# Out projection to MLP in a hybrid decoder block: token tiles one by one, norm gains on DVE, a fixed order on three engines, up blocks two at a time

## Chip, cores and metric

The kernel runs on one core of a Trainium2 chip. The metric is the device time of one execution in microseconds (us). Engines: PE (matmul), DVE (vector), ACT (activation), POOL (GpSimd) and SP, which issues the DMAs.

## What is computed

Two decoder layers on x of 512 tokens by 1024. The stage that the change touches lies between the attention heads and the MLP:

```python
mix = jnp.concatenate([o_fox, o_nsa, o_dil], axis=-1)      # 512 x 1024
x = x + rms_norm(mix @ w_out[l], attn_post_norm[l])
h = rms_norm(x, ffn_pre_norm[l])
x = x + rms_norm(conv_ffn(h, w_up[l], conv_w[l], conv_b[l], w_down[l]), ffn_post_norm[l])

def rms_norm(x, g):
    return x * lax.rsqrt(jnp.mean(x * x, axis=-1, keepdims=True) + RMS_EPS) * g
def conv_ffn(h, w_up, conv_w, conv_b, w_down):
    a, b = jnp.split(causal_depthwise_conv3(h @ w_up) + conv_b, 2, axis=-1)   # 2 x 2816 columns
    return (jax.nn.silu(a) * b) @ w_down
```

## The kernel before

Tokens are worked on in four tiles `s` of 128 (`NST`). Every fp32 matmul is split: an operand is parted into a high half (a copy rounded to fp32r, made by ACT) and a low half (the rest, a subtraction on DVE or POOL), and three products are accumulated: high by high, high by low, low by high.

**Weights.** `plan` lists all weight blocks in order, `getw` (L204) loads (SP) and parts them (`part_weights`, L139) some blocks ahead of use: `ahead` is how far it loads, `pre` how far it parts. Raw blocks, high halves and low halves have three slots each (`wpool`); blocks in `UPS` take their halves from the pool `big` (24 slots of 4 KB per partition), which also holds x, h, the partial out projection `part`, the gains, and the transposed operands `hT`. Blocks in `ONPOOL` are parted in two halves, with POOL for the low half; the others with DVE. An up block (i, n) is 1024 x 128 of w_up; n counts four blocks of one i.

**Out projection.** `part[s]` holds the first half of the heads' products. Four more k (4 to 7) are accumulated in PSUM (`out_mms`, L850): tiles 0 and 1 in the fill of the attention loop, tile 2 and tile 3 at the end (L1207 to L1209). Each tile has two PSUM tiles of 512 columns, `po[s, 0]` and `po[s, 1]`, from four tags ("acc" three banks, "s" two, "pt" two, "o" one).

**Norm and residual.** `mid_post(s)` (L862) loads x for tile s, adds `po` to `part` on DVE (L871) and calls `post_sq` (L275): ACT squares with a row sum (L284), and the gain product h = part x gain (L287) runs on POOL, for all eight halves (`GM1`). `post_r` (L289) and `rstd_of` (L232) give the reciprocal root for a pair of tiles at once: a root on ACT (L234), then on DVE v, a reciprocal, a Newton step (L235 to L243). `post_x` (L300) makes x + h r on DVE (L304) and squares it on ACT (L309). `pre_h` (L311) scales x by its own reciprocal root, on DVE (L322) for all four tiles here (`HA1` is empty) and on ACT (L320) elsewhere for some.

**Turn.** `turn_pair` (L258) transposes two tiles of h on PE (L264; 16 transposes into four PSUM tiles, two k in each), and for each k ACT writes the high half with the pre-norm gain (L269, `hh`) and DVE the low half (L270, `hl`).

**First up blocks.** The four blocks of i = 0 are worked in two halves of 256 tokens (L1230 to L1235): for each pair of k all four blocks in turn, into PSUM tiles acc, acc, s, s; the second turn lies between the halves. The rest of the MLP (L1248 on) takes 512 tokens at a time.

**Order.** Only PE's instructions are held to the program's order (`tc.manual_schedule`, L1183). The order on DVE, ACT, POOL and SP is chosen when the program is built: by what is ready in its scheduler's estimate, with program order as the priority. On the chip each engine then runs its list strictly in that order. So x of tile 3 can be loaded after weights that stand later in the code.

The lines around the change in short:

```python
mid_post(0); mid_post(1); post_r(0); post_x(0); post_x(1)
mid_post(2); pre_h(0, HA1); pre_h(1, HA1)
ws = [getw(l, "up", 0, n, ahead=0) for n in range(2)]
turn_pair(0, 1, l, HT1)
mid_post(3); post_r(1); post_x(2); post_x(3)
ws += [getw(l, "up", 0, n, ahead=UPA[n - 2], pre=UPP[n - 2]) for n in range(2, 4)]
pre_h(2, HA1); pre_h(3, HA1)
```

Of the kernel before, what the change touches and what calls it, by code (L numbers as in the profile page):

```python
# [12 lines left out]
AF = mybir.ActivationFunctionType  # L13
# [5 lines left out]
DM = 1024  # L19
# [10 lines left out]
ONPOOL = ("dv", "dq", "dk", "ks", "nq0", "kw", "kc", "nq1",  # L30
          (0, "fk", 0), (0, "fk", 1), ("up", 0, 1), ("up", 0, 2), ("up", 0, 3), ("up", 1, 0))
PRE = 1
# [11 lines left out]
ORDER = (0, 1, 2, 4, 3, 5, 6, 7, 8)  # L44
GM1 = ((0, 0), (0, 1), (1, 0), (1, 1), (2, 0), (2, 1), (3, 0), (3, 1))
HA0 = (1, 3)
HA1 = ()
XC = 1
# [3 lines left out]
UPS = ((0, 0), (1, 0))  # L52
UPA = (1, 2)
UPP = (0, 1)
HT3 = ("pt", "pt", "acc", "o")
KT = 8


# [18 lines left out]
def tile_hybrid_block(  # L77
# [144 lines left out]
    epsc = const.tile([128, 1], F32, name="epsc")  # L222
    nc.vector.memset(epsc, EPS)
    onec = const.tile([128, 1], F32, name="onec")
# [6 lines left out]

    def rstd_of(total):  # L232
        y, v, t, r = (st(total.shape[-1]) for _ in range(4))
        nc.scalar.activation(y, total, AF.Sqrt, scale=1.0 / DM, bias=epsc)  # L234
        nc.vector.tensor_scalar(v, total, 1.0 / DM, EPS, op0=ALU.mult, op1=ALU.add)  # L235
        nc.vector.reciprocal(y, y)
        if total.shape[-1] == 1:
            nc.vector.scalar_tensor_tensor(t, y, v, y, op0=ALU.mult, op1=ALU.mult)
        else:
            nc.vector.tensor_mul(t, y, v)  # L240
            nc.vector.tensor_mul(t, t, y)
        nc.vector.tensor_scalar(t, t, -0.5, 1.5, op0=ALU.mult, op1=ALU.add)
        nc.vector.tensor_mul(r, y, t)  # L243
        return r

    def new_hT():
# [11 lines left out]
    def turn_pair(half, i, l, tags, tilewise=False):  # L258

        gain = pre_g[:, i, l, :]  # L260
        pts = [ps(tag) for tag in tags]
        order = [(k, i) for k in range(KT) for i in range(2)]
        for k, i in sorted(order, key=lambda z: z[1]) if tilewise else order:
            nc.tensor.transpose(pts[k // 2][:, 256 * (k % 2) + 128 * i:256 * (k % 2) + 128 * i + 128],  # L264
                                hs[2 * half + i][:, 128 * k:128 * k + 128], ident)
        for k in range(KT):
            src = pts[k // 2][:, 256 * (k % 2):256 * (k % 2) + 256]
            hi, lo = (z[k // 2][:, k % 2, 256 * half:256 * half + 256] for z in hT)
            nc.scalar.activation(hi, src, AF.Copy, scale=gain[:, k:k + 1])  # L269
            nc.vector.scalar_tensor_tensor(lo, src, gain[:, k:k + 1], f(hi), op0=ALU.mult, op1=ALU.subtract)  # L270
# [157 lines left out]
    for l in range(DEPTH):  # L428
# [432 lines left out]

        def mid_post(s):  # L862
            if s == 0:
                table(AF.Sqrt, units[-1]["row"][:, 0:1])
            xt = bt([128, DM], name="x")
            nc.sync.dma_start(xt, x[0, 128 * s:128 * s + 128, :] if l == 0 else xsv[128 * s:128 * s + 128, :])
            xs.append(xt)
            y = store["part"][s]
            halves = [y[:, 512 * u:512 * u + 512] for u in range(2)]
            for u in range(2):  # L870
                nc.vector.tensor_add(halves[u], halves[u], po[s, u])  # L871
            post_sq(s, halves, gains[0], GM1)

# [296 lines left out]
        def up_mms(p, w, sl, first, last, ks=range(KT)):  # L1170
            hi, lo = w
            for k in ks:
                mm(p[:, sl], hi[:, k, :], HH(k)[:, sl], first and k == 0, False)
                mm(p[:, sl], hi[:, k, :], HL(k)[:, sl], False, False)
                mm(p[:, sl], lo[:, k, :], HH(k)[:, sl], False, last and k == KT - 1)

# [6 lines left out]
        with tc.manual_schedule(engines={mybir.EngineType.PE}):  # L1183
# [16 lines left out]
            while whole or live[0] or pieces.late:  # L1200
                if whole and store.get("pc"):
                    cmp_values(whole.pop(0)[0])
                elif live[0] or pieces.late:
                    step()
                    chain_step()

            out_mms(2, (7,), True, (0,))  # L1207
            out_mms(2, (4, 5, 6, 7), True, (1,))
            out_mms(3, (4, 5, 6, 7), True)  # L1209
            hT = new_hT()  # L1210
            mid_post(0)
            mid_post(1)
            post_r(0)
            post_x(0)
            post_x(1)
            mid_post(2)
            pre_h(0, HA1)
            pre_h(1, HA1)
            ws = [getw(l, "up", 0, n, ahead=0) for n in range(2)]
            turn_pair(0, 1, l, HT1)  # L1220
            mid_post(3)
            post_r(1)
            post_x(2)
            post_x(3)
            ws += [getw(l, "up", 0, n, ahead=UPA[n - 2], pre=UPP[n - 2]) for n in range(2, 4)]
            pre_h(2, HA1)
            pre_h(3, HA1)
            table(AF.Silu, hs[3][:, 0:1])
            pts = [ps(t) for t in ("acc", "acc", "s", "s")]
            for half in range(2):  # L1230
                if half == 1:
                    turn_pair(1, 1, l, HT3)
                for k in range(0, KT, 2):
                    for n in range(4):
                        up_mms(pts[n], ws[n], slice(256 * half, 256 * half + 256), half == 0, half == 1, (k, k + 1))  # L1235

# [102 lines left out]
```

## Time and profile before

| | us |
|---|---|
| median of 3 runs (lowest to highest) | 1391.84 (1391.26 to 1394.37) |
| the profiled execution, its time | 1393.86 |
| its span, first to last instruction | 1391.9 |
| PE busy | 1341.9 (96%) |
| DVE busy | 869.6 (62%) |
| ACT busy | 725.5 (52%) |
| POOL busy | 316.4 (23%) |

All durations come from the one profiled execution. The stage in question occurs once per layer, in the trace near 314 to 361 us and near 1000 to 1047 us. "Busy" of PE says that matmuls were in flight, not that they ran at full speed; the granted clock of PE is 1.00 at 2.4 GHz and 0.50 at 1.2 GHz. A timeline row gives start, duration, engine, line, operation, output <- inputs, shape and count; a row with a count above one covers several instructions in a row. In brackets stands how long the engine was idle before it, and whose result ended that. In the names, `wh`, `wl` are high and low weight halves (`wh_up`, `wl_up`: those with wpool slots), `sm` small columns of sums and roots.

### The profile page before, as it was taken

Reading aid. Unit: us, or ns where it says so; the run is one execution under the profiler, and the core shown is the slowest. Engines: PE = TensorE matmul, PEld = TensorE weight load, DVE = VectorE, ACT = ScalarE, POOL = GpSimd, SP = SyncE. Lnnn points to the kernel's source line nnn. Section 1 sums busy time; section 2 is a strip of 40 time slices with the busy share of each in tenths; the row PEclk is TensorE's granted clock in tenths of the full one; section 3 lists DMA queues with packets and bytes.
Section 4 is the critical chain, followed back from the end, with each engine's and each line's share of the span. In section 5 each row is a group of like instructions: output and inputs, shape, how many; then the busy total and the mean of one; then the engine's idle time right before and its main releaser. Section 6 shows DMA issues by size and latency. Waiting matters only on the chain.

```text
span 1391.9 us, 21204 instructions
## 1 busy us (share of the span) xinstructions
PE 1341.9 (96%) x7835; PEld 1181.3 (85%) x7835; DVE 869.6 (62%) x2006; ACT 725.5 (52%) x1525; POOL 316.4 (23%) x363
## 2 busy tenths in 40 slices
PE   6999999998999999999999999999989999999997
PEld 5899998977888888888899899999788888888886
DVE  6678877678655555533464887876767555554334
ACT  6567766775443333423465677677655333333232
POOL 2363763345000000000004646633430000000000
PEclk9999999999999999999999999999999999999999
DMA  5224311132233333223323143112323333332231
GB/s 178 77 62 116 102 46 37 54 122 63 77 91 100 98 92 106 91 96 124 117 81 105 47 125 88 32 46 62 106 61 101 96 92 105 91 103 95 91 121 61
DMA packets 145519, 123.75 MB, mean 89 GB/s; under 512 B 8264, under 2 KB 135688, under 8 KB 145416
## 3 DMA queue, kind: packets, MB, share of 16 engines
q1 hardware_dynamic: 145416, 122.40, 29.1%
q8 instruction: 62, 1.02, 0.3%
q14 instruction: 41, 0.34, 0.1%
HBM read 118.19 MB, written 4.19 MB: 88 GB/s over the span
## 4 chain that ended last, share of the span: by engine, by line
PE 80%; DVE 11%; ACT 6%; issue 2%; DMA 0%; POOL 0%; SPq 0%; ACTq 0%; DVEq 0%
PE acc L117 36%; PE s L117 18%; PE pt L117 13%; PE o L117 10%; PE pt L1102 3%; DVE hl L270 1%; DVE wt L772 1%; DVE x L304 1%; DVE pl L1118 1%; DVE r L1077 1%; DVE r L449 1%; ACT r L284 1%; DVE h L322 1%; ACT r L1082 1%; PE pt L714 1%
## 5 line engine op out<-in xcount | busy, mean ns | idle before, releaser
L156 DVE TENSOR_TENSOR wl_up<-raw_up,wh_up 128x1024 fp32r<-128x1024 f32 x78 | 95.6, 1225 | 163.1 <-ACT wh_up L148 163.1
L148 ACT ACTIVATE wh_up<-raw_up 128x1024 fp32r<-128x1024 f32 (+1 forms) x90 | 89.6, 1002 | 154.3 <-PE acc L117 68.1
L156 DVE TENSOR_TENSOR wl_wd<-raw_wd,wh_wd 128x1024 fp32r<-128x1024 f32 x42 | 51.5, 1226 | 133.6 <-ACT wh_wd L148 133.6
L148 ACT ACTIVATE wh_wd<-raw_wd 128x1024 fp32r<-128x1024 f32 x42 | 44.5, 1061 | 144.9 <-PE pt L117 135.5
L1082 ACT ACTIVATE r<-r,sm 128x128 f32<-128x128 f32 x192 | 106.7, 557 | 21.5 <-DVE sm L1077 20.8
L1089 POOL TENSOR_SCALAR r<-r,sm,gates 128x128 f32<-128x128 f32 (+3 forms) x128 | 86.6, 682 | 119.4 <-DVE sm L1087 82.6
L152 POOL TENSOR_TENSOR wl_kc<-raw_kc,wh_kc 128x512 fp32r<-128x512 f32 x8 | 12.0, 1511 | 419.5 <-ACT wh_kc L148 418.7
L117 PE MATMUL acc<-hh,wh_up 128*128 128x512 f32 (+1 forms) x272 | 102.4, 377 | 0.0
L117 PE MATMUL acc<-hl,wh_up 128*128 128x512 f32 (+1 forms) x272 | 102.4, 377 | 0.0
L117 PE MATMUL acc<-hh,wl_up 128*128 128x512 f32 (+1 forms) x272 | 102.4, 376 | 0.0
L117 PE MATMUL s<-k,q 128*128 128x512 f32 (+3 forms) x384 | 96.5, 338 | 2.2 <-DVE sm L1077 0.9
L1118 DVE TENSOR_TENSOR pl<-pt,ph 128x384 fp32r<-128x384 f32 x144 | 85.6, 595 | 16.9 <-ACT ph L1113 15.5
L1113 ACT ACTIVATE ph<-pt 128x384 fp32r<-128x384 f32 x144 | 75.4, 524 | 24.7 <-PE pt L1102 23.1
L1077 DVE CUSTOM_DVE_ANT_0 r<-s,cmask 128x128 f32<-128x128 f32 (+3 forms) x160 | 75.8, 483 | 18.3 <-PE s L117 13.4
L1102 PE MATMUL pt<-ident,r 128*128 128x128 f32 x480 | 77.9, 277 | 7.2 <-DVE pl L1118 5.7
L117 PE MATMUL acc<-wh_wd,gh 128*128 128x512 f32 x252 | 83.7, 389 | 0.0
L117 PE MATMUL s<-hh,wh_up 128*128 128x512 f32 (+1 forms) x224 | 80.6, 360 | 2.2 <-DVE hl L270 2.2
L117 PE MATMUL s<-hl,wh_up 128*128 128x512 f32 (+1 forms) x224 | 80.3, 359 | 0.0
L117 PE MATMUL s<-hh,wl_up 128*128 128x512 f32 (+1 forms) x224 | 80.3, 359 | 0.0
L1263 ACT ACTIVATE r<-r 128x512 f32<-128x512 f32 x44 | 27.8, 633 | 81.3 <-DVE r L1244 81.0
L1102 PEld LDWEIGHTS pt<-ident,r 128*128 128x128 f32 x480 | 55.7, 141 | 16.1 <-POOL r L1089 7.1
L117 PE MATMUL acc<-wh_wo,mix 128*128 128x256 f32 (+1 forms) x296 | 67.5, 305 | 0.0
(431 smaller groups left out, 4187.2 us busy)
## 6 DMA issues: line engine op xcount, KB each, us to landing
raw_up<-in_w_up_dram SPq DMA_DIRECT2D x88, 512.0 KB, 3.8
raw_wd<-in_w_down_dram SPq DMA_DIRECT2D x44, 512.0 KB, 3.4
raw_wo<-in_w_out_dram SPq DMA_DIRECT2D x16, 512.0 KB, 3.4
x<-in_x_dram SPq DMA_DIRECT2D x8, 512.0 KB, 6.5
raw_nq<-in_w_in_dram SPq DMA_DIRECT2D x8, 512.0 KB, 3.6
raw_w<-in_cmp_w_k_dram SPq DMA_DIRECT2D x8, 512.0 KB, 3.7
raw_w<-in_cmp_w_v_dram SPq DMA_DIRECT2D x8, 512.0 KB, 4.2
raw_fk<-in_w_in_dram SPq DMA_DIRECT2D x4, 512.0 KB, 6.8
```

The source lines that it names most:

```text
L117: nc.tensor.matmul(o, lhsT=lhsT, rhs=rhs, start=start, stop=stop, skip_group_check=True)
L148: nc.scalar.activation(hi[:, ks], raw[:, ks], AF.Copy)
L156: nc.vector.tensor_sub(lo[:, ks], raw[:, ks], f(hi)[:, ks])
L270: nc.vector.scalar_tensor_tensor(lo, src, gain[:, k:k + 1], f(hi), op0=ALU.mult, op1=ALU.subtract)
L284: nc.scalar.activation(scr, y, AF.Square, accum_out=stats["p", s // 2][:, c:c + 1])
L1077: nc.vector.tensor_tensor_reduce(row[:, 0:n], u["S"][:, 0:n], u["mask"][:, 512 - n:512], op0=ALU.add, op1=ALU.min, scale=1.0, scalar=3.0e3 ...
L1082: nc.scalar.activation(row[:, 0:n], row[:, 0:n], AF.Exp, scale=-1.0, bias=sm_[:, 0:1], accum_out=sm_[:, 1:2])
L1089: nc.gpsimd.tensor_scalar(row[:, 0:n], row[:, 0:n], sm_[:, 2:3], g_, op0=ALU.mult, op1=ALU.mult)
L1102: nc.tensor.transpose(p[:, 128 * c:128 * c + 128], blocks[z], ident)
L1113: nc.scalar.activation(hi, src, AF.Copy)
L1118: nc.vector.tensor_sub(*u["lo"])
L1263: nc.scalar.activation(cd[0], cd[0], AF.Silu)
```

## The change

The post-norm and pre-norm work is taken tile by tile for tiles 0 and 1, with a sum and a reciprocal root for each tile (tiles 2 and 3 still share the first one); the gain products move from POOL to DVE; h of tiles 0 and 2 is scaled on ACT, of 1 and 3 on DVE. PE, DVE and ACT are held to program order from the last out-projection matmuls to the end of the first four up blocks. Transposes go tile by tile, the evacuation of k goes 0, 2, 1, 3, 4, 6, 5, 7 in every turn of the kernel, and the up matmuls follow that order, blocks 0 and 1 through all k before blocks 2 and 3. The x loads and the h tiles come earlier, the parts of up blocks (0,2) and (0,3) come before the first turn, and block (1,0) is parted by ACT and DVE behind the second turn instead of by POOL. The reciprocal root has one DVE operation fewer everywhere (constants are folded by a factor of four).

```diff
-          (0, "fk", 0), (0, "fk", 1), ("up", 0, 1), ("up", 0, 2), ("up", 0, 3), ("up", 1, 0))
+          (0, "fk", 0), (0, "fk", 1), ("up", 0, 1), ("up", 0, 2), ("up", 0, 3))
...
+KORDER = (0, 2, 1, 3, 4, 6, 5, 7)
...
-    def rstd_of(total):
-        y, v, t, r = (st(total.shape[-1]) for _ in range(4))
-        nc.scalar.activation(y, total, AF.Sqrt, scale=1.0 / DM, bias=epsc)
-        nc.vector.tensor_scalar(v, total, 1.0 / DM, EPS, op0=ALU.mult, op1=ALU.add)
+    def rstd_begin(total):
+
+        y, v = (st(total.shape[-1]) for _ in range(2))
+        nc.scalar.activation(y, total, AF.Sqrt, scale=4.0 / DM, bias=epsc)
+        nc.vector.tensor_scalar(v, total, -4.0 / DM, -4.0 * EPS, op0=ALU.mult, op1=ALU.add)
+        return y, v
+
+    def rstd_end(y, v):
+        t, r = (st(y.shape[-1]) for _ in range(2))
         nc.vector.reciprocal(y, y)
...
-        nc.vector.tensor_scalar(t, t, -0.5, 1.5, op0=ALU.mult, op1=ALU.add)
-        nc.vector.tensor_mul(r, y, t)
+        nc.vector.scalar_tensor_tensor(r, t, 3.0, y, op0=ALU.add, op1=ALU.mult)
         return r
...
-        for k in range(KT):
+        for k in KORDER:
             src = pts[k // 2][:, 256 * (k % 2):256 * (k % 2) + 256]
...
+        def mid_load(s):
             xt = bt([128, DM], name="x")
             nc.sync.dma_start(xt, x[0, 128 * s:128 * s + 128, :] if l == 0 else xsv[128 * s:128 * s + 128, :])
             xs.append(xt)
...
+            hs.append(bt([128, DM], name="h"))
+
+        def mid_add(s, u, square=True):
+
+            y = store["part"][s][:, 512 * u:512 * u + 512]
+            nc.vector.tensor_add(y, y, po[s, u])
+            if square:
+                mid_square(s, u)
+
+        def mid_square(s, u):
+            y = store["part"][s][:, 512 * u:512 * u + 512]
+            nc.scalar.activation(rt(), y, AF.Square, accum_out=mid["p"][:, s % 2 + 2 * (s // 2) + 4 * u:][:, 0:1])
+
+        def mid_gain(s, us=(0, 1)):
+            for u in us:
+                cs = slice(512 * u, 512 * u + 512)
+                nc.vector.tensor_mul(hs[s][:, cs], store["part"][s][:, cs], gains[0][:, cs])
+
+        def mid_total(s, n=1):
+            tot = st(n, "sx")
+            nc.vector.tensor_add(tot, mid["p"][:, s:s + n], mid["p"][:, 4 + s:4 + s + n])
+            return rstd_begin(tot)
+
+        def mid_x(s, r):
+            nc.vector.scalar_tensor_tensor(xs[s], hs[s], r, xs[s], op0=ALU.mult, op1=ALU.add)
+            nc.scalar.activation(hs[s], xs[s], AF.Square, accum_out=mid["x"][:, s:s + 1])
...
+            for s in range(2):
+                mid_load(s)
+            ws = [getw(l, "up", 0, n, ahead=0) for n in range(2)]
+
+
+        table(AF.Sqrt, units[-1]["row"][:, 0:1])
+        mid["p"], mid["x"] = st(8, "sq"), st(4, "sx")
+        for s in range(2, NST):
+            mid_load(s)
+        with tc.manual_schedule(engines={mybir.EngineType.PE, mybir.EngineType.DVE, mybir.EngineType.Activation}):
             out_mms(2, (7,), True, (0,))
             out_mms(2, (4, 5, 6, 7), True, (1,))
             out_mms(3, (4, 5, 6, 7), True)
             hT = new_hT()
...
+            mid_add(0, 0)
+            mid_add(0, 1)
+            mid_gain(0)
+            a0 = mid_total(0)
+            mid_add(1, 0)
+            mid_x(0, rstd_end(*a0))
+            mid_add(1, 1)
+            mid_gain(1)
+            b0 = rstd_begin(mid["x"][:, 0:1])
+            a1 = mid_total(1)
+            nc.scalar.activation(hs[0], xs[0], AF.Copy, scale=rstd_end(*b0))
+            mid_x(1, rstd_end(*a1))
+            mid_add(2, 0)
+            mid_gain(2, (0,))
+            b1 = rstd_begin(mid["x"][:, 1:2])
+            mid_add(2, 1)
+            nc.vector.tensor_scalar(hs[1], xs[1], rstd_end(*b1), None, op0=ALU.mult)
+            ws.append(getw(l, "up", 0, 2, ahead=1, pre=0))
+            ws.append(getw(l, "up", 0, 3, ahead=2, pre=0))
+            mid_add(3, 0, False)
+            mid_add(3, 1, False)
+            mid_gain(2, (1,))
+            turn_pair(0, 1, l, HT1, True)
+            mid_square(3, 0)
+            mid_square(3, 1)
+            mid_gain(3)
+            r = rstd_end(*mid_total(2, 2))
+            mid_x(2, r[:, 0:1])
+            mid_x(3, r[:, 1:2])
+            for s in range(2, 4):
+                r = rstd_of(mid["x"][:, s:s + 1])
+                if s == 2:
+                    nc.scalar.activation(hs[s], xs[s], AF.Copy, scale=r)
+                else:
+                    nc.vector.tensor_scalar(hs[s], xs[s], r, None, op0=ALU.mult)
             table(AF.Silu, hs[3][:, 0:1])
             pts = [ps(t) for t in ("acc", "acc", "s", "s")]
             for half in range(2):
                 if half == 1:
-                    turn_pair(1, 1, l, HT3)
-                for k in range(0, KT, 2):
-                    for n in range(4):
-                        up_mms(pts[n], ws[n], slice(256 * half, 256 * half + 256), half == 0, half == 1, (k, k + 1))
+                    turn_pair(1, 1, l, HT3, True)
+                    getw(l, "up", 1, 0, ahead=1, pre=0, peek=True)
+                for n0 in (0, 2):
+                    for k in range(0, KT, 2):
+                        for n in (n0, n0 + 1):
+                            up_mms(pts[n], ws[n], slice(256 * half, 256 * half + 256), half == 0, half == 1,
+                                   KORDER[k:k + 2])
```

## Rows read from the trace of the kernel before

**Rows 1.** The page, part 4: the chain that ended last, by engine.

```profile
PE 80%; DVE 11%; ACT 6%; issue 2%; DMA 0%; POOL 0%; SPq 0%; ACTq 0%; DVEq 0%
```

**Rows 2.** Windows: length, busy time of each engine (instructions), granted clock, DMA share, GB/s.

```profile
329.40:333.10 3.70, 3.48 (x18) 3.22 (x19) 2.45 (x6) 3.04 (x9) 3.70 (x3) 0.57 0.02 4
...
333.10:344.90 11.80, 10.70 (x87) 10.35 (x87) 10.09 (x20) 6.68 (x15) 6.63 (x6) 1.00 0.59 178
...
332.50:333.00 0.50, 0.50 (x6) 0.50 (x5) 0.50 (x2) 0.50 (x2) 0.50 (x1) 0.93 0.00 0
...
1015.40:1019.10 3.70, 3.47 (x17) 3.22 (x18) 2.44 (x6) 3.04 (x9) 3.70 (x3) 0.56 0.02 4
```

**Rows 3.** Timeline of PE: start, us, operation, count [idle before <- releaser].

```profile
326.76 0.39 PE L117 MATMUL acc<-wh_wo,mix 128*128 128x512 f32 x1
...
329.38 0.45 PE L264 MATMUL pt<-ident,h 128*128 128x128 f32 x1 [2.23 <-DVE h L322]
...
330.04 1.73 PE L264 MATMUL pt<-ident,h 128*128 128x128 f32 x7 [0.22 <-DVE h L322]
...
332.85 0.36 PE L117 MATMUL acc<-hh,wh 128*128 128x256 f32 x1
...
336.63 0.36 PE L117 MATMUL s<-hh,wh_up 128*128 128x256 f32 x1 [0.60 <-DVE hl L270]
...
346.53 0.98 PE L264 MATMUL pt<-ident,h 128*128 128x128 f32 x7 [0.20 <-DVE h L322]
...
360.57 0.40 PE L117 MATMUL pt<-hh,wh 128*128 128x512 f32 x1
```

**Rows 4.** The chain of waits in order of time: start, us, what.

```profile
350.65 1.44 PE s L117 x12
...
1386.28 0.16 DVE sm L242
...
1386.66 1.28 DVE x L304
```

**Rows 5.** Timeline of POOL.

```profile
315.04 5.05 POOL L287 TENSOR_TENSOR h<-part,gain 128x512 f32<-128x512 f32 x4 [9.61 <-DVE part L871]
...
321.64 2.27 POOL L287 TENSOR_TENSOR h<-part,gain 128x512 f32<-128x512 f32 x1 [1.55 <-DVE part L871]
```

**Rows 6.** Timeline of DVE.

```profile
314.26 2.05 DVE L871 TENSOR_TENSOR part<-part,acc 128x512 f32<-128x512 f32 x3 [0.38 <-PE acc L117]
...
318.89 1.22 DVE L235 TENSOR_SCALAR sm<-sm 128x2 f32<-128x2 f32 x1
...
321.48 3.52 DVE L304 SCALAR_TENSOR_TENSOR x<-h,sm,x 128x1024 f32<-128x1024 f32 x2
...
328.48 1.42 DVE L322 TENSOR_SCALAR h<-x,sm 128x1024 f32<-128x1024 f32 x2
...
332.43 0.88 DVE L270 SCALAR_TENSOR_TENSOR hl<-pt,preg,hh 128x256 fp32r<-128x256 f32 x2 [0.16 <-ACT hh L269]
...
364.63 0.68 DVE L1264 TENSOR_TENSOR g<-r,r 128x512 f32<-128x512 f32 x1
```

**Rows 7.** Timeline of ACT.

```profile
318.89 0.30 ACT L234 ACTIVATE sm<-sm,epsc 128x2 f32<-128x2 f32 x1 [1.06 <-DVE sm L293]
...
322.79 1.06 ACT L309 ACTIVATE h<-x 128x1024 f32<-128x1024 f32 x1 [0.47 <-DVE x L304]
...
328.64 1.66 ACT L148 ACTIVATE wh_up<-raw_up 128x512 fp32r<-128x512 f32 x3
...
330.95 0.47 ACT L269 ACTIVATE hh<-pt,preg 128x256 fp32r<-128x256 f32 x1 [0.66 <-PE pt L264]
```

**Rows 8.** Timeline of SP's DMA queue.

```profile
306.94 1.05 SPq L866 DMA_DIRECT2D x<-in_x_dram  x2
...
332.71 0.58 SPq L866 DMA_DIRECT2D x<-in_x_dram  x1
```

**Rows 9.** The page, part 6: DMA issues, KB each, median us to landing.

```profile
raw_up<-in_w_up_dram SPq DMA_DIRECT2D x88, 512.0 KB, 3.8
```

More of the change, by code (lines that the diff above doesn't have):

```diff
@@ L44 @@
 ORDER = (0, 1, 2, 4, 3, 5, 6, 7, 8)
-GM1 = ((0, 0), (0, 1), (1, 0), (1, 1), (2, 0), (2, 1), (3, 0), (3, 1))
 HA0 = (1, 3)
-HA1 = ()
 XC = 1
@@ L52 @@
 UPS = ((0, 0), (1, 0))
-UPA = (1, 2)
-UPP = (0, 1)
 HT3 = ("pt", "pt", "acc", "o")
 KT = 8
+KORDER = (0, 2, 1, 3, 4, 6, 5, 7)
 PAT = ((0,), (2, 1), (4, 5, 3), (6, 9, 7, 8))
@@ L222, in tile_hybrid_block @@
     epsc = const.tile([128, 1], F32, name="epsc")
-    nc.vector.memset(epsc, EPS)
+    nc.vector.memset(epsc, 4.0 * EPS)
     onec = const.tile([128, 1], F32, name="onec")
@@ L230, in table @@
         nc.scalar.activation(t, after, func, scale=0.0, bias=onec)
-    def rstd_of(total):
-        y, v, t, r = (st(total.shape[-1]) for _ in range(4))
-        nc.scalar.activation(y, total, AF.Sqrt, scale=1.0 / DM, bias=epsc)
-        nc.vector.tensor_scalar(v, total, 1.0 / DM, EPS, op0=ALU.mult, op1=ALU.add)
+    def rstd_begin(total):
[5 more added lines that the diff above has]
+        t, r = (st(y.shape[-1]) for _ in range(2))
         nc.vector.reciprocal(y, y)
-        if total.shape[-1] == 1:
+        if y.shape[-1] == 1:
             nc.vector.scalar_tensor_tensor(t, y, v, y, op0=ALU.mult, op1=ALU.mult)
@@ L241, in rstd_of @@
             nc.vector.tensor_mul(t, t, y)
-        nc.vector.tensor_scalar(t, t, -0.5, 1.5, op0=ALU.mult, op1=ALU.add)
-        nc.vector.tensor_mul(r, y, t)
-        return r
+        nc.vector.scalar_tensor_tensor(r, t, 3.0, y, op0=ALU.add, op1=ALU.mult)
+        return r
+    def rstd_of(total):
+        return rstd_end(*rstd_begin(total))
     def new_hT():
@@ L860, in tile_hybrid_block @@
         hs.clear()
-        def mid_post(s):
-            if s == 0:
-                table(AF.Sqrt, units[-1]["row"][:, 0:1])
+        def mid_load(s):
             xt = bt([128, DM], name="x")
@@ L867, in mid_post @@
             xs.append(xt)
[L868 to L872, printed above, removed]
+            hs.append(bt([128, DM], name="h"))
[18 more added lines that the diff above has]
+            nc.scalar.activation(hs[s], xs[s], AF.Square, accum_out=mid["x"][:, s:s + 1])
+        mid = {}
         def out_start():
@@ L1172, in up_mms @@
             for k in ks:
-                mm(p[:, sl], hi[:, k, :], HH(k)[:, sl], first and k == 0, False)
+                mm(p[:, sl], hi[:, k, :], HH(k)[:, sl], first and k == KORDER[0], False)
                 mm(p[:, sl], hi[:, k, :], HL(k)[:, sl], False, False)
-                mm(p[:, sl], lo[:, k, :], HH(k)[:, sl], False, last and k == KT - 1)
+                mm(p[:, sl], lo[:, k, :], HH(k)[:, sl], False, last and k == KORDER[-1])
         RATE = [1.4] * 12 + [0.8] * 98
@@ L1210, in tile_hybrid_block @@
             hT = new_hT()
[L1211 to L1227, printed above, removed]
+            mid_add(0, 0)
[33 more added lines that the diff above has]
+                    nc.vector.tensor_scalar(hs[s], xs[s], r, None, op0=ALU.mult)
             table(AF.Silu, hs[3][:, 0:1])
```

## The prediction

> **What bounds the kernel now.** I read the chain that ended last first: TensorE (PE) holds 80% of the span, DVE 11% and ACT 6% [rows 1]. So a saving counts only where PE waits or runs slowly. Then the stage that the diff touches, cut into windows, once per layer, and PE's timeline in it. The layers agree to 0.1 us (the slow stretch gave PE 3.48 of 3.70 us at a granted clock of 0.57 in one, 3.47 of 3.70 at 0.56 in the other) [rows 2], so I work out layer 0 and take it twice.
>
> The last out-projection matmul starts at 326.76 and ends at 327.15; the first matmul of the next pair of up blocks starts at 360.57 [rows 3]: 33.4 us. The work in it is 192 up matmuls (two halves, 8 k, 4 blocks, 3 products), at 12 in 1.44 us [rows 4] 23.0 us, and 32 transposes, at 7 in 0.98 us [rows 3] at most 4.5 and nearer 4: together 27. About 6.4 us per layer can be won. They go to: 2.23 us before the first transpose, for DVE's h; the clock, which falls to half (1.2 GHz) after that idle time, so that 16 transposes take the 3.70 us window instead of some 2.0; 1.10 us in the window from 333.1 (11.80 long, 10.70 busy) [rows 2], where blocks 2 and 3 wait until DVE has emptied the PSUM tiles that they take over (0.60 us before the second of them); the rest around the two turns (first operands of each half, 0.20 us for h before the second) [rows 3].
>
> Why h is late is in DVE's and POOL's rows. POOL multiplies the norm gains, four in 5.05 us from 315.04 [rows 5]. While it does, tiny DVE operations that take 0.16 us elsewhere [rows 4] take 1.22, and two updates of x, 1.28 each at the kernel's end [rows 4], take 3.52 [rows 6]: they take turns with POOL.
>
> **The change, part by part.** The start is the same: DVE's first addition at 314.26, when PE delivers [rows 6].
>
> *DVE up to h1.* In the new order DVE does, tile by tile: for tile 0 two additions (0.68, three in 2.05) and two gain products (bounded by the same-shaped product of two SBUF operands, 0.68; 1.27, POOL's own time, as the far bound; I take 0.66 in a row, since it is DVE's own row [rows 6]): 2.6; one addition, 0.7; five small ones at 0.2 apart, 1.0; the x update, 1.28; an addition and two products, 2.0; eight small ones, 1.6; an x update, 1.28; two additions and a product of tile 2, 2.0; four small ones, 0.8; h1's scaling, 0.71 (two in 1.42, ending at 329.9 before) [rows 6]. Sum 13.9: h1 at 328.1. ACT's squares (1.06 for a whole tile [rows 7], some 0.6 for half of one, and a short reading of the sum behind each) fall beside it, and h0, which ACT scales in 1.06, is ready near 323.7, not 329.2. No POOL work is left in this stretch, so nothing makes DVE's operations wait; that is where the 5 us that DVE takes over are paid.
>
> *First turn.* PE transposes h0 from 327.2 without a gap, then h1 from about 328.2 to 329.3. ACT's fixed order puts the four weight halves of up blocks 2 and 3 (three in 1.66 [rows 7], so 2.2) after its last square, at 327.4, and ahead of the evacuation, so the first hh starts at 329.7, before 330.95 [rows 7]. With 0.47 for hh and 0.44 for hl (two in 0.88) [rows 6, 7] both operands of the first k stand at 330.6; before, the first up matmul started at 332.85 [rows 3]. The gain is 2.3. Here lies the clock's gain too: PE's longest idle time shrinks from 2.23 to about 1 us, so I take the full clock; at half, 1.7 comes back.
>
> *Evacuation order.* The order that goes round the tiles lets ACT fill the next tile while DVE reads the last. Two blocks a time use a pair of k in 1.44 us, for which ACT and DVE need some 0.9, so PE doesn't starve, and blocks 2 and 3 start 5.8 us later, when their PSUM tiles are long empty. The 1.10 us are gone. Half 0 ends at 330.6 + 95 x 0.12 = 342.0.
>
> *Second half.* Now DVE and ACT are late next. DVE's last hl of half 0 ends near 333.6. Then two gain products, 1.4, with 0.2 for a meeting with POOL's last half (335.2); sum and reciprocal root of both tiles, 1.2; two x updates, 2.56 (339.0); ACT's second square to 340.2; root (0.30 [rows 7]) and three small ones, 0.9; ACT's scaling of h2, 1.06 (342.2); root and small ones for h3, behind it on ACT, 0.9; scaling, 0.71 (343.8); one transposed column block, hh and hl, 1.1: 344.9. PE has transposed h2 by then. End of half 1: 345.0 + 11.5 = 356.5 to 356.6, against 360.57: **4.0 us per layer**, 8.0 for two. Some 2.4 of the 6.4 stay lost.
>
> *Block (1,0).* Its weight part goes from POOL to ACT and DVE, behind the second turn, done by about 350, needed at 356.6: nothing. If that cover went it would cost PE at most the 4.0 gained.
>
> *Loads.* The x loads and the tiles for h come earlier in SP's queue and in the pool; before, two x loads went out at 306.94 and the fourth only at 332.71 [rows 8]. They are needed at 318 to 338: nothing, if slots are free (see the slower rival).
>
> *Reciprocal root.* One small DVE operation fewer wherever it is used. On the chain that is sure at the tail (0.16 and its gap, 0.2 [rows 4]) and at the layer boundary, 0.2; at the start between 0 and 0.4; I take 0.4 in all. The turns elsewhere only change the order of k: between -0.5 and +0.5 by one operand's 0.44 and its gap; I take 0, the middle, for DVE and ACT are not held to program order there.
>
> Sum: 8.0 + 0.4 = 8.4. The profiled execution took 1393.86 us (span 1391.9 and 2.0 around it), so it would take 1385.5. The median of the runs is 2.0 lower, 1391.84, which gives **1383.4**.
>
> **The rivals.** *The clock falls all the same* (15%). Between 327.15 and the first up matmul near 330.2 PE has only transposes, with gaps. If these keep no clock up, PE starts the up matmuls at half speed, and the 1.7 us come back in both layers: 1386.8. Against it: the clock was back within the window from 332.50 (mean 0.93, so by 332.6) [rows 2], when PE had run nothing but transposes since 329.38; the first matmul came at 332.85 [rows 3].
>
> The Trainium skill (TensorE: Matmul & The Clock Gate, Part 4: PE-mode transpose) says that a transpose "doesn't count as PE-busy the same way"; by that rule the time would be this rival's, and the trace disagrees, with the clock back before any matmul.
>
> *The fixed order turns POOL's work into waits* (10%). The parts of blocks 2 and 3 on POOL now run from about 328 to 333.5, and DVE's gain products of tiles 2 and 3 stand ahead of hl and of h2. If each of two meetings costs a whole POOL operation (1.27), 2.5 per layer: 1388.4. For it: the 1.22 us operations. Against: they wait for at most one operation, and POOL is nearly done at tile 3.
>
> *Given back downstream* (8%). If the weights of the second pair of blocks keep their old times, PE waits there for all it won: 1391.4. Against it: blocks 0 and 1 end 5.8 us before the stage does, and free their weight tiles and PSUM earlier.
>
> *Slower: the queue behind x* (5%). The x loads of tiles 2 and 3 now stand ahead of the weights of up blocks 2 and 3. If x3 still finds its slot at 332.71 and SP holds those weights behind it, they issue at 333.3 and 333.8 and land 3.8 later [rows 9], ACT has them parted at 338.7 and hh follows in ACT's order: 9.0 late, less the 4.0, is 5.0 per layer slower, 1401.4. It decides once the last weights land after 334. Against it: before, three h tiles had slots by 321.7 [rows 5], which is enough for h0, h1 and x3 now.
>
> **How the numbers follow.** Forecast 62%. A measurement of this kernel tells about 0.2% (2.8 us) from no change. Faster: forecast, clock and half of the POOL case, which lies on the bound: 0.82. Same: the other half and the downstream case, 0.13. Slower: 0.05. The forecast's own range is 1380.0 (another 1.7 per layer, from the first evacuation at once after h1 and from the second half's chain) to 1386; with the clock and the POOL case it reaches 1388.5. What is left out is the last two rivals and little below.
>
> **What would show it.** Right: POOL idle between 315 and 328; DVE's small operations below 0.2 us there; h1 near 14 us after the first addition; no half clock in this stage; no wait between blocks 1 and 2; the stage, from the last out-projection matmul to the next pair of up blocks, near 29.5 us, and PE without gaps after it. Wrong: a stage above 31.5 us, ACT waiting in front of the weight halves, an x load landing after its update is due, or a stage that shrank while the next blocks wait.

## The result, and the profile after

The kernel after takes 1383.64 us (median of 5 runs, 1382.12 to 1385.29); the kernel before took 1391.84 (5 runs, 1390.17 to 1394.37). The ratio is 0.9941, 95% interval [0.9927, 0.9956]: 8.2 us faster, where 8.4 were forecast. Once more, on another chip: 1384.44 against 1391.36, 0.9942 [0.9925, 0.9958]. The profiled execution took 1385.29 us (span 1383.5).

Below, **the stage** runs from the start of the last out-projection matmul to the start of the next pair of up blocks; before, that was 33.81 us in layer 0 (360.57 less 326.76 [rows 3]) and 33.85 in layer 1. On this measure the forecast was 29.9 (29.5, and the 0.39 of the last matmul). It is now 29.21 in both. PE's timeline after, layer 0, to be held against [rows 3]:

```profile
330.06 0.39 PE L114 MATMUL acc<-wh_wo,mix 128*128 128x512 f32 x1
...
331.60 0.60 PE L268 MATMUL s<-ident,h 128*128 128x128 f32 x4
...
332.75 0.38 PE L114 MATMUL acc<-hh,wh 128*128 128x256 f32 x1 [0.56 <-ACT hh L273]
...
346.23 0.66 PE L268 MATMUL pt<-ident,h 128*128 128x128 f32 x4 [0.38 <-DVE h L1279]
...
359.26 0.40 PE L114 MATMUL pt<-hh,wh 128*128 128x512 f32 x1
```

The transposes follow the out projection without a gap; the first up matmul starts 2.3 us after the last out-projection matmul ends (5.7 before); no wait is left between the blocks, and two waits of 0.56 and 0.38 us remain. The windows of the stage after (columns as in [rows 2]):

```profile
330.45:332.75 2.30, 1.75 (x17) 1.51 (x14) 2.15 (x5) 2.27 (x6) 2.03 (x2) 1.00 0.03 7
332.75:344.30 11.55, 11.41 (x92) 11.22 (x93) 8.73 (x23) 7.68 (x18) 3.49 (x3) 1.00 0.31 91
344.30:348.00 3.70, 3.18 (x25) 2.60 (x24) 2.09 (x6) 3.13 (x7) 0.00 (x0) 1.00 0.00 0
...
1010.04:1012.34 2.30, 1.75 (x17) 1.51 (x14) 2.15 (x5) 2.27 (x6) 2.03 (x2) 1.00 0.01 4
```

The granted clock is 1.00 throughout, where it was 0.57 and 0.56. DVE's timeline after answers to [rows 6]:

```profile
317.57 1.37 DVE L875 TENSOR_TENSOR part<-part,acc 128x512 f32<-128x512 f32 x2 [0.38 <-PE acc L114]
318.85 1.29 DVE L886 TENSOR_TENSOR h<-part,gain 128x512 f32<-128x512 f32 x2
...
321.36 0.16 DVE L244 SCALAR_TENSOR_TENSOR sm<-sm,sm 128x1 f32<-128x1 f32 x1
321.55 1.28 DVE L894 SCALAR_TENSOR_TENSOR x<-h,sm,x 128x1024 f32<-128x1024 f32 x1
...
330.04 0.75 DVE L1261 TENSOR_SCALAR h<-x,sm 128x1024 f32<-128x1024 f32 x1
...
332.73 0.87 DVE L274 SCALAR_TENSOR_TENSOR hl<-pt,preg,hh 128x256 fp32r<-128x256 f32 x2
...
344.77 0.16 DVE L238 RECIPROCAL sm<-sm 128x1 f32<-128x1 f32 x1 [1.34 <-ACT sm L232]
...
345.42 0.75 DVE L1279 TENSOR_SCALAR h<-x,sm 128x1024 f32<-128x1024 f32 x1
```

The gain products cost DVE 1.29 for two, as taken; the small operations are back at 0.16, and h1 is done 13.2 us after the first addition (13.9 forecast). ACT's timeline answers to [rows 7], POOL's to [rows 5], SP's to [rows 8]; here are the three after:

```profile
325.57 1.15 ACT L1255 ACTIVATE h<-x,sm 128x1024 f32<-128x1024 f32 x1 [0.41 <-DVE sm L244]
...
330.02 2.18 ACT L145 ACTIVATE wh_up<-raw_up 128x512 fp32r<-128x512 f32 x4
332.23 0.84 ACT L273 ACTIVATE hh<-pt,preg 128x256 fp32r<-128x256 f32 x2
...
344.46 0.28 ACT L232 ACTIVATE sm<-sm,epsc 128x1 f32<-128x1 f32 x1
```

```profile
330.72 5.52 POOL L149 TENSOR_TENSOR wl_up<-raw_up,wh_up 128x512 fp32r<-128x512 f32 x4 [22.00 <-ACT wh_up L145]
```

```profile
307.63 2.30 SPq L868 DMA_DIRECT2D x<-in_x_dram  x4
```

POOL is idle for the 22 us in which h0 and h1 are made. All four x loads go out at 307.63, so none is late. The chain that ended last has PE at 81% and DVE at 9%, in place of 80 and 11 [rows 1].

### The profile page after: what moved, and what is told of

Read it like the earlier page. It is cut to its first block, busy times and chain, and to the rows that moved or that the text cites. A ratio compares the mean times of both kernels' runs of the same rounds, so it can differ in the third digit from the quotient of the medians.

```text
span 1383.5 us, 21191 instructions
## 1 busy us (share of the span) xinstructions
PE 1338.9 (97%) x7835; PEld 1179.5 (85%) x7835; DVE 866.7 (63%) x2021; ACT 732.1 (53%) x1533; POOL 289.0 (21%) x343
## 3 DMA queue, kind: packets, MB, share of 16 engines
q8 instruction: 62, 1.02, 0.3%
## 4 chain that ended last, share of the span: by engine, by line
PE 81%; DVE 9%; ACT 6%; issue 1%; DMA 1%; POOL 1%; SPq 0%; ACTq 0%; DVEq 0%
PE acc L114 37%; PE s L114 19%; PE pt L114 12%; PE o L114 10%; PE pt L1127 3%; DVE wt L776 1%; DVE r L1102 1%; DVE pl L1143 1%; DVE hl L274 1%; ACT r L1107 1%; DMA raw_up<-in_w_up_dram 1%; DVE r L453 1%; PE pt L718 1%; ACT hh L273 0%; ACT r L1176 0%
```

## The experiments

The stage is the same to 0.2 us in both layers of most traces, while whole runs of one kernel scatter over 3 us and more. So the stage decides, and the time is its check. Ratios are against the kernel before, run beside each.

| kernel | stage, layers 0 and 1, us | clock 1.2 GHz in the stage | median us | ratio [95%] |
|---|---|---|---|---|
| before | 33.81, 33.85 | both layers | 1391.84 | 1 |
| after | 29.21, 29.21 | no | 1383.64 | 0.9941 [0.9927, 0.9956] |
| after: gain products on POOL | 34.51, 33.53 | both | 1394.36 | 1.0017 [1.0007, 1.0028] |
| after: only PE in fixed order | 33.12, 32.91 | both | 1392.76 | 0.9997 [0.9988, 1.0006] |
| after: four blocks in turn | 30.14, 30.15 | no | 1387.08 | 0.9964 [0.9951, 0.9976] |
| after: plain k order | 31.91, 31.91 | no | 1387.9 | 0.9966 [0.9953, 0.9978] |
| after: block (1,0) with POOL | 29.21, 29.23 | no | 1384.0 | 0.9938 [0.9918, 0.9959] |
| after: h2, h3 on DVE | 28.62, 28.61 | no | 1383.47 | 0.9944 [0.9928, 0.9959] |
| the same, again | 28.62, 28.63 | no | 1383.3 | 0.9933 [0.9916, 0.995] |
| after, again | 29.23, 29.24 | no | 1384.44 | 0.9942 [0.9925, 0.9958] |
| before: gain products on DVE | 32.57, 32.47 | layer 0 only | 1389.2 | 0.9978 [0.9966, 0.999] |
| before: fixed order | 49.06, 49.15 | both, twice each | 1422.11 | 1.0218 [1.02, 1.0237] |
| before: new root | 33.70, 33.72 | layer 0 only | 1392.0 | 0.9996 [0.9982, 1.001] |
| before: filler transposes | 41.43, 41.91 | both, late | 1407.06 | 1.0107 [1.0092, 1.0123] |

### Undoing one part of the change

**The gain products back on POOL.**

```diff
-                nc.vector.tensor_mul(hs[s][:, cs], store["part"][s][:, cs], gains[0][:, cs])
+                nc.gpsimd.tensor_mul(hs[s][:, cs], store["part"][s][:, cs], gains[0][:, cs])
```

> The changed kernel with the eight gain products on POOL again and everything else kept. Theory (POOL's products hold up DVE and arrive late): each pair of products takes 2.54 us on POOL instead of 1.29 on DVE, and DVE, held to program order, waits for them before each x update and loses up to 1.27 us at small operations; h1 is 2 to 4 us later after the first addition than the 13.2 us of the changed kernel, and the total is 4 to 8 us above the changed kernel (1387 to 1392). Rival (what counts is the tile-by-tile order, the engine of the products is indifferent): within 1.5 us of the changed kernel.

All of the gain goes, and more. DVE's list, POOL's, and PE's in this kernel show why:

```profile
328.51 1.11 DVE L240 SCALAR_TENSOR_TENSOR sm<-sm,sm 128x1 f32<-128x1 f32 x1
329.66 1.24 DVE L244 SCALAR_TENSOR_TENSOR sm<-sm,sm 128x1 f32<-128x1 f32 x1
330.94 1.72 DVE L1261 TENSOR_SCALAR h<-x,sm 128x1024 f32<-128x1024 f32 x1
```

```profile
326.98 2.63 POOL L886 TENSOR_TENSOR h<-part,gain 128x512 f32<-128x512 f32 x2 [3.29 <-DVE part L875]
329.62 5.42 POOL L149 TENSOR_TENSOR wl_up<-raw_up,wh_up 128x512 fp32r<-128x512 f32 x4
```

```profile
332.80 1.08 PE L268 MATMUL pt<-ident,h 128*128 128x128 f32 x4 [4.42 <-DVE h L1261]
```

Three operations that take 0.22, 0.16 and 0.75 without POOL take 4.1 together beside it, all on h1's chain; PE stands 4.42 us and then runs its transposes at half speed (1.08 for four, not 0.60). The products stand in the way, as the theory says, and by more: h1 ends 18.0 us after the first addition, 4.8 later than in the kernel after where 2 to 4 was expected, and the time lies above the 1387 to 1392. Only the first of the three stands beside the products; made late by them, the other two meet POOL's weight subtractions as well.

**Only PE in program order**; DVE and ACT are listed by the scheduler.

```diff
-        with tc.manual_schedule(engines={mybir.EngineType.PE, mybir.EngineType.DVE, mybir.EngineType.Activation}):
+        with tc.manual_schedule(engines={mybir.EngineType.PE}):
```

> The changed kernel with DVE and ACT no longer held to program order in this stage (PE still is). Theory (the gain lies in the tile-by-tile work, the products on DVE and the pairs of blocks): the scheduler finds nearly the same order, and the total is within 2 us of the changed kernel. Rival (the fixed order is what gives the gain): the total is 4 us or more above it, with DVE or ACT doing something else ahead of h0 and h1.

The theory fell, and the rival holds: the fixed order is needed. DVE's list, PE's and POOL's:

```profile
331.84 0.69 DVE L875 TENSOR_TENSOR part<-part,acc 128x512 f32<-128x512 f32 x1 [1.02 <-PE acc L114]
...
333.33 1.19 DVE L244 SCALAR_TENSOR_TENSOR sm<-sm,sm 128x1 f32<-128x1 f32 x1
334.56 1.72 DVE L1261 TENSOR_SCALAR h<-x,sm 128x1024 f32<-128x1024 f32 x1
```

```profile
336.33 0.66 PE L268 MATMUL pt<-ident,h 128*128 128x128 f32 x4 [3.66 <-DVE h L1261]
```

```profile
332.00 5.40 POOL L149 TENSOR_TENSOR wl_up<-raw_up,wh_up 128x512 fp32r<-128x512 f32 x4 [21.93 <-ACT wh_up L145]
```

The list puts an addition for tile 3 ahead of h1's chain. It waits 1.02 us for PE, and by then POOL has started on the weights, so h1 meets it after all: it ends 4.87 us after the start of the last out-projection matmul (331.41), against 0.73 in the kernel after. The order's worth is that h1 is done when POOL's next work begins (330.79 and 330.72 in the kernel after).

**All four blocks in turn**, as before.

```diff
-                for n0 in (0, 2):
+                for n0 in (0,):
...
-                        for n in (n0, n0 + 1):
+                        for n in range(4):
```

> The changed kernel with all four up blocks in turn for each pair of k, as before the change. Theory: blocks 2 and 3 wait for the PSUM tiles of the first turn again; the evacuation of the last k ends at about 336.4 in the trace of the changed kernel and blocks 2 and 3 would be due 1.44 us after the first up matmul (334.8), so 1 to 1.7 us of PE waits per half 0; but the second half starts when h of tile 3 is there (346.2), 1.4 us after PE ends half 0, so all but 0 to 0.5 us per layer is hidden: 0 to 1 us above the changed kernel. Rival (the 1.1 us per layer come back in full): 2 to 3 us above it.

0.93 us per layer by the stage: nearer the rival. The wait for the PSUM tiles that the evacuation still holds is back, before the third block's first matmul:

```profile
336.57 0.35 PE L114 MATMUL s<-hh,wh_up 128*128 128x256 f32 x1 [1.33 <-DVE hl L274]
```

Half 0 takes 1.54 us longer. The second turn takes up 0.6 of them, where the wait for h3 is gone; the rest is the stage's loss.

**The plain order of k.**

```diff
-KORDER = (0, 2, 1, 3, 4, 6, 5, 7)
+KORDER = (0, 1, 2, 3, 4, 5, 6, 7)
```

> The kernel after, with the operands of a turn taken in the order k = 0, 1, 2 to 7 in place of the order that goes round the shared tiles. Theory (ACT's write of hh for the odd k waits until DVE has read the same tile for the even one, so a k costs about 0.95 us in place of 0.47 in each turn): 2 to 5 us per layer, 1388 to 1394, with ACT's hh waiting for DVE's hl and PE waiting for hh at both turns. Rival (readers of one tile don't hold up each other, or PE has operands in hand): within 1 us of the kernel after.

2.70 us per layer, as the theory has it. ACT's list and DVE's in the first turn:

```profile
330.88 0.84 ACT L273 ACTIVATE hh<-pt,preg 128x256 fp32r<-128x256 f32 x2 [0.55 <-DVE hl L274]
```

```profile
331.39 0.88 DVE L274 SCALAR_TENSOR_TENSOR hl<-pt,preg,hh 128x256 fp32r<-128x256 f32 x2 [0.54 <-ACT hh L273]
```

ACT waits for DVE and DVE for ACT, half a us each time. The evacuation of half 0 takes 6.3 us (first hh at 329.86, last hl done at 336.13), against 4.2 in the order that goes round the tiles (332.23 to 336.45), and the second half's chain starts 2 us later; the rest of the 2.7 is the second turn's.

**Block (1,0) parted with POOL again.**

```diff
-          (0, "fk", 0), (0, "fk", 1), ("up", 0, 1), ("up", 0, 2), ("up", 0, 3))
+          (0, "fk", 0), (0, "fk", 1), ("up", 0, 1), ("up", 0, 2), ("up", 0, 3), ("up", 1, 0))
```

> The kernel after, with block (1,0) parted with POOL again in place of ACT and DVE. Theory (the block is needed only at the end of the stage, so it does not matter who parts it): the stage 29.2 us in both layers, the time within 0.6 us of the kernel after. Rival (POOL's subtractions fall on DVE's small operations of tiles 2 and 3 and hold up h3): 1 to 3 us per layer slower, with DVE operations above 1 us before h3.

Nothing changes: POOL takes it at 351.61, 4.9 us after h3 is done (346.73).

### Doing one part alone in the kernel before

**The gain products on DVE alone** (GM1 empty).

```diff
-GM1 = ((0, 0), (0, 1), (1, 0), (1, 1), (2, 0), (2, 1), (3, 0), (3, 1))
+GM1 = ()
```

> The kernel before, with the gain products of the stage on DVE and nothing else changed; DVE, ACT and POOL keep the order that the scheduler lists. Theory (neither the products' engine nor the order gives the gain alone; without a held order the lists put work of later tiles ahead of what PE waits for): within 1.5 us of the kernel before, 1390 to 1394, and the half clock still falls in the stage in both layers. Rival (POOL's products standing in the way of DVE's small operations are the whole cause, so moving them is enough): 2 to 5 us per layer faster, below 1388, with no half clock in the stage.

Between the two, so neither bound held: 1.2 and 1.4 us per layer of the 4.6. What was not foreseen is that the clock fell in one layer and not in the other. The last eight transposes of the turn in both, from PE's timeline:

```profile
331.45 1.91 PE L264 MATMUL s<-ident,h 128*128 128x128 f32 x8
...
1014.24 1.04 PE L264 MATMUL s<-ident,h 128*128 128x128 f32 x8
```

Yet the stages are 32.57 and 32.47: at full speed PE waited for hh and hl instead (0.24, 0.34 and 0.45 us).

**The fixed order alone**: PE, DVE and ACT held to the old program order.

```diff
+        with tc.manual_schedule(engines={mybir.EngineType.PE, mybir.EngineType.DVE, mybir.EngineType.Activation}):
             out_mms(2, (7,), True, (0,))
```

> The kernel before, with PE, DVE and ACT held to its own program order from the last out-projection matmuls to the end of the first four up blocks; the products stay on POOL. Theory (a fixed order alone gives nothing; this program order has tile 2's additions and both tiles' roots in pairs, and POOL's products stand in it): the same as the kernel before or slower, 1391 to 1400. Rival (the fixed order alone is what gives the gain): 4 us or more faster, below 1388.

15 us per layer slower, far beyond both bounds. PE's list shows two waits that the old program order builds in:

```profile
337.03 0.50 PE L117 MATMUL acc<-hh,wh_up 128*128 128x256 f32 x1 [3.48 <-DVE part L871]
...
345.29 0.58 PE L117 MATMUL s<-hh,wh_up 128*128 128x256 f32 x1 [6.69 <-ACT wh_up L148]
```

Tile 3's additions stand behind the turn, and their PSUM tile is wanted by block 1; the weight halves of blocks 2 and 3 stand behind the squares of x2 and x3. The change pulls both ahead of the turn. A fixed order is worth what is written in it.

**The new reciprocal root alone.**

```diff
-        nc.vector.tensor_scalar(t, t, -0.5, 1.5, op0=ALU.mult, op1=ALU.add)
-        nc.vector.tensor_mul(r, y, t)
+        nc.vector.scalar_tensor_tensor(r, t, 3.0, y, op0=ALU.add, op1=ALU.mult)
```

> The kernel before, with the reciprocal root that has one DVE operation fewer, and nothing else. Theory (the root is on the path only at the tail and at the layer boundary): 0.4 to 1.2 us below the kernel before, with both places shorter by 0.2 to 0.6 us each and the stage as before at 33.8 us. Rival (the scheduler lists DVE's work otherwise): the stage changes by more than 0.5 us in one layer at least, and the time by more than 1.5 us.

The layer boundary is 0.40 us shorter (a stretch of 100 matmuls there takes 15.07 us, not 15.47), and the next 100 take 0.2 less, the same as in every kernel with this root; the time does not tell it from no change. DVE's list did change, and this made a clean test of the clock. In both layers the first up matmul comes 4.62 us after the stage starts, 1.5 sooner than before, and then the windows of the stage differ:

```profile
333.30:336.80 3.50, 3.50 (x19) 3.50 (x19) 3.28 (x9) 3.12 (x8) 3.50 (x4) 0.55 0.89 293
...
1017.10:1020.60 3.50, 3.06 (x23) 2.66 (x22) 3.28 (x9) 3.10 (x8) 3.50 (x4) 1.00 0.90 292
```

Half the clock in layer 0, full clock and idle time in layer 1, and stages of 33.70 and 33.72. The last matmul of half 0 starts 19.50 us into the stage in layer 0 and 19.00 in layer 1. Then layer 1 waits for h3, and layer 0 does not:

```profile
345.64 1.04 PE L271 MATMUL pt<-ident,h 128*128 128x128 f32 x8
...
1029.49 0.98 PE L271 MATMUL pt<-ident,h 128*128 128x128 f32 x7 [0.30 <-DVE h L329]
```

So half 1 begins at 21.29 and 21.30 us. Neither the clock nor the earlier start was worth anything here, since the second half begins when h3 is there, and DVE and ACT (3.28 and 3.1 of 3.5 us busy in both windows) make it.

**Filler transposes** in PE's gap: 20 transposes of the gain tile into an unused PSUM tile.

```diff
             out_mms(3, (4, 5, 6, 7), True)
+            fill_ = ps("pt")
+            for i in range(20):
+                nc.tensor.transpose(fill_[:, 128 * (i % 4):128 * (i % 4) + 128], gains[0][:, 128 * (i % 8):128 * (i % 8) + 128], ident)
```

> The kernel before with 20 transposes of the gain tile put into PE's idle time behind the last out-projection matmul of each layer (their result is not used). Theory (transposes keep the clock up, and the idle time alone let it fall): no half clock in this stage, the 16 transposes of h take about 2 us instead of 3.7, 1.4 to 1.7 us less per layer: 2.5 to 3.5 us below the kernel before, stage 31.7 to 32.2 instead of 33.4. Rival (transposes do not count): the clock falls all the same, the total is within 1 us of the kernel before or up to 0.6 above it.

PE's timeline answers the question on transposes, and shows why the time says nothing on it:

```profile
326.13 2.35 PE L1212 MATMUL pt<-ident,gain 128*128 128x128 f32 x20
...
329.98 1.04 PE L264 MATMUL s<-ident,h 128*128 128x128 f32 x8
...
338.33 0.58 PE L117 MATMUL acc<-hl,wh 128*128 128x256 f32 x1 [5.64 <-DVE hl L270]
```

With nothing but transposes since the out projection, the turn's last eight run at full speed (1.04, where the same eight took 1.91 in the list above at half speed). But the scheduler listed DVE's work anew, the root and x update of tiles 2 and 3 ahead of hl, and PE stood 5.64 us behind them. The low clock of this kernel comes only in that wait (from 334.17), and its stage, with the 20 transposes in it, takes 41.43 us.

### A better order for the second half

**h2 and h3 both on DVE**: both updates of x in a row, each root on ACT behind its own square.

```diff
-            mid_x(2, r[:, 0:1])
-            mid_x(3, r[:, 1:2])
             for s in range(2, 4):
-                r = rstd_of(mid["x"][:, s:s + 1])
-                if s == 2:
-                    nc.scalar.activation(hs[s], xs[s], AF.Copy, scale=r)
-                else:
-                    nc.vector.tensor_scalar(hs[s], xs[s], r, None, op0=ALU.mult)
+                nc.vector.scalar_tensor_tensor(xs[s], hs[s], r[:, s - 2:s - 1], xs[s], op0=ALU.mult, op1=ALU.add)
+            nc.scalar.activation(hs[2], xs[2], AF.Square, accum_out=mid["x"][:, 2:3])
+            b2 = rstd_begin(mid["x"][:, 2:3])
+            nc.scalar.activation(hs[3], xs[3], AF.Square, accum_out=mid["x"][:, 3:4])
+            nc.vector.tensor_scalar(hs[2], xs[2], rstd_end(*b2), None, op0=ALU.mult)
+            nc.vector.tensor_scalar(hs[3], xs[3], rstd_of(mid["x"][:, 3:4]), None, op0=ALU.mult)
```

> The kernel after, with the end of the second half's chain in another order: both updates of x on DVE in a row, then on ACT square of x2, root 2, square of x3, root 3; h2 and h3 are both scaled on DVE. In the trace of the kernel after root 3 stands on ACT behind the scaling of h2 (1.15 us), and DVE waits 1.34 us for it. Theory (the second half is bound by this chain): h3 some 1.5 us earlier, PE without a wait at the second turn, 1.0 to 1.4 us per layer, 2 to 3 us below the kernel after. Rival (PE has the second half's work in hand whatever h3 does, or the squares take the place of the wait): within 0.6 us of the kernel after.

In the kernel after, root 3 stood on ACT at 344.46, behind h2's scaling. Here DVE no longer waits for it; from DVE's list of this kernel:

```profile
338.75 0.75 DVE L1277 TENSOR_SCALAR h<-x,sm 128x1024 f32<-128x1024 f32 x1
...
340.12 0.75 DVE L1278 TENSOR_SCALAR h<-x,sm 128x1024 f32<-128x1024 f32 x1
```

Its last out-projection matmul starts at 326.45, so h3 ends 14.4 us into the stage, not 16.1. PE has no wait at the second turn, and the stage is 0.6 us shorter per layer; the rest of h3's 1.7 us is slack. That is about half of the 1.0 to 1.4 expected. The medians didn't settle it, so both kernels ran once more on one chip.

> The kernel after, unchanged, on the chip of the other runs of this call, as the measure for the kernel with h2 and h3 on DVE. Expected: 8 us below the kernel before, 1383 to 1385; in the trace the stage (start of the last out-projection matmul to start of the next pair of up blocks) 29.2 us in both layers as in its first trace, and half clocks in the attention at other places or none.

> The kernel with h2 and h3 on DVE once more, beside the kernel after on the same chip. Theory (its trace showed the stage at 28.62 us in place of 29.21 in both layers, and nothing else changed): 1.2 us below the kernel after in the medians, within about 1 us either way for the half clocks that fall at random in the attention. Rival (the 0.6 us per layer are given back later): the same as the kernel after to 0.3 us, with a longer time in the later part of each layer.

The stages repeat (28.62 against 29.23), and the medians are 1.1 us apart, as the theory has it, though the intervals overlap. Up to the layer boundary nothing is given back (1475 matmuls from the stage's end in 334.55 us in both). Whether something is given back in layer 1's attention stays open: matmuls 4200 to 6122 took 273.1 us in both traces of this kernel, with two low-clock stretches, and 271.2 and 269.6 in the two of the kernel after, with one and none. It is the fastest kernel of the study by its traces; by its times it is level with the kernel after or a little below.

## Why the prediction was right, and where not

*The stage, 4.0 us per layer forecast, 4.6 measured.* h1's chain held step by step (13.2 for 13.9, whose terms add up to 13.97; h0 ready 9.15 us after the first addition, for 9.4). The first up matmul came 2.30 us after the out projection, not 3.45. About 0.8 of this is ACT: its weight halves start 12.45 us after the first addition, not 13.14, and hh starts 1.78 us after the out projection, not 2.55. The other 0.4 is a wait that doesn't exist: the prediction let the matmul wait for both operands of the first k, and it needs hh alone. That carries through half 0, and h3 came 15.7 us after the out projection, for 16.65.

*The clock.* The rival "the clock falls all the same" fell: from 330.45 to 332.75 PE ran only transposes and then waited 0.56 us, the granted clock was 1.00, and no low clock follows in the stage, in either layer of either trace. The Trainium skill (TensorE: Matmul & The Clock Gate, Part 4: PE-mode transpose) says that a transpose doesn't count as PE-busy the same way; the kernel after and the filler's 1.04 us disagree with it. The rival's price, 1.7 us per layer, no run of the kernel after shows. In kernels near the one before it was far smaller: two had the low clock in one layer and not in the other, and paid 0.1 us at most. So "here lies the clock's gain too" counted a limit of the kernel before as a loss, while another limit stood behind it. Where PE waits for nothing the low clock does cost: with the products on POOL, half 0 has no wait in either layer, the low clock lasts to 11.35 us into the stage in layer 0 and to 9.03 in layer 1, and the stages are 34.51 and 33.53. Windows of that kernel, layer 0 and layer 1, columns as in [rows 2]:

```profile
335.00:338.40 3.40, 3.40 (x18) 3.40 (x18) 2.58 (x6) 3.19 (x9) 2.51 (x3) 0.50 0.63 174
1021.20:1024.60 3.40, 3.40 (x31) 3.40 (x30) 2.21 (x10) 2.38 (x7) 1.30 (x2) 1.00 0.52 150
```

*Evacuation order and block pairs.* "The 1.10 us are gone" is right: the pairs are worth 0.93, the k order 2.70. Undone singly, the products (4.3 to 5.3, with the low clock that came along), the list order (3.7 to 3.9), the k order (2.7) and the pairs (0.9) add up to 11.6 to 12.8 us of a gain of 4.6; done singly, products, order and root give 1.2 to 1.4, minus 15, and 0.1. So they are links of one chain: removing one uncovers the next. The prediction summed over one path, which is why its stage term came within 0.6 us where a sum of the parts would not.

*The fixed order* had no term of its own; the prediction took its effect as the order's as written. The run with only PE held shows that it is needed, and the old order held shows that it is not enough.

*The POOL case* didn't occur: in the kernel after two hl take 0.88 at most beside POOL's subtractions, as before [rows 6]; tile 2's second product takes 0.69 among them, at 331.90, and it is POOL that loses there (its four in 5.52, where one takes 1.29); and the gain products of tile 3 start as POOL ends. *Given back downstream*: no; from the stage to the layer boundary both kernels take 334.55 us for the same 1475 matmuls. *The queue behind x*: no.

*Block (1,0) at nothing*: right, by its own run.

*The root, 0.4*: the boundary gives 0.40 alone and 0.2 right behind it (matmuls 4000 to 4200 in 30.94 us before and 30.75 after), and the tail went from 8.04 to 7.41 us from the last matmul's start; its old-root kernels lie from 7.61 to 8.04 and its new-root kernels from 7.41 to 7.86, so how much of the tail is the root's stays open.

*"The turns elsewhere only change the order of k ... I take 0"* is the step that failed. In layer 0's attention, matmuls 400 to 800 took 52.59 us before and 54.98 after. In the six traces with the plain order they took 52.55 to 52.77; in the eight with the new one 53.67 to 53.71 where the clock stayed up, and 54.98 to 55.10 where it fell. It begins with one meeting; DVE and POOL of the kernel after:

```profile
87.83 1.10 DVE L453 TENSOR_TENSOR r<-rope,rope 128x32 f32<-128x32 f32 x1 [0.23 <-issue]
```

```profile
87.59 1.29 POOL L149 TENSOR_TENSOR wl_nq<-raw_nq,wh_nq 128x512 fp32r<-128x512 f32 x1
```

the same two products in the kernel after with the plain order of k and nothing else changed:

```profile
86.86 0.30 DVE L453 TENSOR_TENSOR r<-rope,rope 128x32 f32<-128x32 f32 x2
```

and PE's next transposes there, in the kernel after and in the one with the plain order of k:

```profile
100.16 1.11 PE L718 MATMUL pt<-ident,r 128*128 128x128 f32 x4 [2.04 <-DVE pl L1143]
```

```profile
98.69 0.66 PE L718 MATMUL pt<-ident,r 128*128 128x128 f32 x4 [1.63 <-DVE pl L1143]
```

With the new order the second of two small products comes just after POOL's subtraction has begun, and ends with it, at 88.93; with the plain order both are done by 87.16. The meeting stands in all eight traces with the new order and in none of the six with the plain one. (Of the 1.47 us between PE's two rows, 0.54 was there at matmul 400.) The low clock, from 100.03 in the kernel after, came in five of the eight and in none of the six. By the traces' stretch 400 to 800, 1.1 us are lost at full clock and 2.4 with the low one. The Trainium skill (SBUF — State Buffer, section SBUF: two separate sides) says that of a DVE operation with two SBUF inputs and a GpSimd operation that reads SBUF the first holds the shared ports for its whole length while the other blocks; this meeting agrees, ending 0.05 us behind POOL's. That the order of k costs the time is shown by the run that changes it alone; that it does so through this meeting is read from the rows, with no run of its own.

The total: 4.61 and 4.64 in the stages, 0.59 at and behind the boundary, 0.63 at the tail, less 2.39 in the attention, 8.1 of the 8.4 us between the two profiled spans; the rest is low-clock stretches that come and go between runs (matmuls 5400 to 5600 in 29.19 us before, with one, and 27.65 after) and small differences both ways. The forecast 8.4 was reached with a stage term 1.2 too small, a term for the boundary and the tail 0.8 too small and an attention term that left out 2.4, which nearly cancel. That the total was met to 0.2 us is therefore luck in good part; that the stage gives the gain, along this path, is not.

An order of k that goes round the tiles in the stage's turns alone, with h2 and h3 on DVE, would by these rows spare 1.1 us more, or 2.4 where the clock falls; this is an estimate, and it was not tried.

## What to carry to other kernels

Cost a stage along one path from its start to its end, and at each wait that you remove ask which wait stands right behind it: here the products on DVE and the held order each take most of the gain along when they go, and neither gives it alone. Read a low clock as a loss only if PE had operands in hand at that time and no later wait takes the loss up. And when a shared helper's order is changed, look at every place that uses it: the gain of 2.7 us per layer in this stage cost up to 2.4 in another.

## What the runs showed of the hardware

A clock of 1.2 GHz for 3.4 us cost the stage nothing measurable where PE waited for operands afterwards (33.70 against 33.72 us), and 2.3 us more of it cost 0.98 where PE waited for nothing (34.51 against 33.53). TensorE's granted clock stayed at 1.00 while it ran only transposes, 20 of them in 2.35 us, and the next 16 at full speed (the last eight in 1.04). A DVE operation that works on one number per partition took 1.1 to 1.24 us, in place of 0.16 to 0.22, beside a POOL product or subtraction of 1.3, and a scaling of 128x1024 took 1.72 in place of 0.75, while DVE's hl, which reads PSUM, was not slowed (0.87 for two). The kernel after had a low clock near 783 us in its first trace and not in its second, which is worth 1.4 us there (matmuls 4400 to 4800 in 55.33 and 53.97 us); its runs scatter by 3.2.
